# Down projection of a bidirectional encoder block: when the operands of the next item are started, and where the outputs of the upper rows stand

## The chip, the cores and the metric

The kernel runs on one core of one Trainium2 chip. The metric is device time in microseconds (us): the median of three runs, and beside it the span of one profiled execution, from its first to its last instruction. The engines are PE (matmul; PEld is its weight load), DVE (vector), ACT (scalar), POOL (GpSimd) and SP, which issues the DMAs. Each engine works through its own instructions in order; an instruction waits until the results and the buffers that it needs are released by the other engines.

## The reference, cut to what matters

One encoder layer is applied to 512 + 256 positions with the same weights. The change touches its last part, the second matrix product of the feed-forward network with the residual, and the final norm:

```
ff_gate, ff_up = jnp.split(n2 @ w_ffn_in[layer].astype(f32), 2, axis=-1)
h = h + (jax.nn.silu(ff_gate) * ff_up) @ w_ffn_out[layer].astype(f32)
...
out = _rmsnorm(h, norm_final_g)
```

Here `h` is 768 x 1024, the gated activation 768 x 2816, and `w_ffn_out` 2816 x 1024, all in float32. `_rmsnorm` divides each row by the root of its mean square and multiplies by a gain.

## The kernel before

**The product.** The 2816 inner positions are 22 blocks of 128, taken as 11 *pairs*. A pair is a 2 x 2 problem: activations a11, a12 (upper 384 rows), a21, a22 (lower 384 rows), weights b11, b12, b21, b22 (128 x 512 each). It is done with seven products instead of eight, called P2, P1, P5, P6, P3, P7, P4 in the order in which they run; most take a sum or difference of blocks as an operand, so sums are formed in place beforehand: the activation sums on POOL (`fr<-fr`, `fback<-fback`, 128 x 384), the weight sums on POOL for P5 and P4 and on DVE for P6 and P7 (`w<-w`, `wraw<-w,wraw`, 128 x 512). Pairs come in two *groups* of six and five; within a group all pairs do P2, then all do P1, and so on. One product of one pair is called an *item* here: 42 items in group 0, 35 in group 1.

**An item.** Each float32 operand is split into a high part in a shorter format and the low remainder. `operands(op)` (L2161) forms the sums and then calls `aconv` and `convert` or `staged`: ACT copies the high parts (`ahi` of the activations, `whi` of the weights), DVE subtracts to get the low parts (`alo`, `wlo`). `staged` (L2127) also has ACT copy the weights into one of two PSUM tiles (`acc<-w`), from which DVE then reads them. PE does nine matmuls per item: three row blocks i, each hi*hi, lo*hi, hi*lo (L82 to L84, or L2274 where a product adds onto earlier ones). `ahi`, `alo`, `whi`, `wlo` have rings of six buffers (AH, WH).

**The order.** `Ops(f2src(), 4)` (L2209) builds operands four items ahead of the one that PE is given: `ops.next()` hands over item n and builds item n+4. After a product's last item the sums are added to the residual rows `hres` by DVE (`accumulate`: `hres<-acc,hres`, three per product). These adds and the work on the norm stand in a queue `late`, of which up to three are emitted after each item (L2304). The upper rows (i = 0, 1, 2) are complete after P3 of group 1, the lower ones after P4. So P3 puts `upper_scales` (three squares on ACT, then a chain of seven small POOL operations that gives the scales `rstd`) and the outputs of the upper rows (`finish`, L2237) into `late`; they are emitted between the items of P7. An output piece (`yq`, 128 x 512) takes an ACT scaling and a POOL multiplication by the gain, or, where `spare` is false, one DVE operation. At the last item of P7 (`at_once`, L2296) DVE adds each row block as soon as PE has finished it, because P4 goes on in the same PSUM tiles: the first matmul of P4 has to wait for that add. P4 of group 1 runs row block by row block over its five items, and each lower row block is finished behind it.

Of the kernel before, what the change touches and what calls it, by code (L numbers as in the profile page):

```python
# [9 lines left out]
F32R = mybir.dt.float32r  # L10
I32 = mybir.dt.int32
AF = mybir.ActivationFunctionType
# [21 lines left out]
WH = 6  # L34
EARLY = (1, 2)
AH = 6
# [25 lines left out]
def build(nc, tc, I, O):  # L62
    V = nc.vector
# [4 lines left out]
    def pool(name, bufs=1, side=None, space=None):  # L68
        kw = {}
        if space is not None:  # L70
            kw["space"] = space
        if side is not None:
            kw["side"] = side
        if space is not DRAM:
            kw["reuse_waits"] = "tile"
        return tc.tile_pool(name=name, bufs=bufs, **kw)

    def raw(t):
        return t.bitcast(F32)
# [9 lines left out]
    def tt(e, out, a, b, op):  # L89
        e.tensor_tensor(out=out, in0=a, in1=b, op=op)  # L90
# [10 lines left out]
    def act(out, a, f, **kw):  # L101
        A.activation(out=out, in_=a, func=f, **kw)  # L102

    C3, C4 = P, P
    MUL, ADD, SUB = ALU.mult, ALU.add, ALU.subtract
# [3 lines left out]
    def enter(cm):  # L109
        p = cm.__enter__()  # L110
        ctx.append(cm)
        return p
# [37 lines left out]
    wk = enter(pool("wk"))  # L150
# [28 lines left out]
    class Ops:  # L179
# [10 lines left out]
        def next(self):  # L190
            self.fill(1)
            w = self.q.popleft()
            self.fill(self.ahead)
            return w
# [414 lines left out]
    rs = {}  # L609
# [735 lines left out]
    def f(n=1):  # L1345
        for _ in range(n):
            next(filler, None)
# [384 lines left out]
    for m in range(KT):  # L1732
        sga = glp.tile([128, 2, 384], F32, name="sga", tag="yr", bufs=2)
        nc.sync.dma_start(out=sga, in_=gascr[m].rearrange("p (b c) -> p b c", b=2))
        w = ws.two()
# [118 lines left out]
    for k in range(KT):  # L1854
        w = ws.next()
# [141 lines left out]
    def h12(i):  # L1997
        return hres[:, i, 512:1024]

    def h21(i):  # L2000
        return hres[:, 3 + i, 0:512]
# [82 lines left out]
    for m in range(KF):  # L2084
# [4 lines left out]
        g = gated(m, fr)  # L2089
# [10 lines left out]
    leave(n2pa_cm)  # L2100
    f2r = enter(pool("f2r", side="right"))

    def ahl():
        return [f2r.tile([128, 384], F32R, name=n, tag=n, bufs=AH) for n in ("ahi", "alo")]

    def fback():
        return f2r.tile([128, NT], F32, name="fback", tag="fback", bufs=SPILL)
# [1 line left out]
    def w21():  # L2109
        return f2r.tile([128, 1024], F32, name="w21", tag="w21", bufs=6)  # L2110

    ahl()
    fback()
    w21()

    def aconv(x, eng):
        hi, lo = ahl()
        act(hi, x, AF.Copy)
        tt(eng, lo, x, raw(hi), SUB)
        return hi, lo  # L2120

    order = list(range(SPILL // 2, KF // 2)) + list(range(SPILL // 2))
    groups = [order[0:6], order[6:11]]
    P2, P1, P5, P6, P3, P7, P4 = range(7)
    stg = []

    def staged(w):  # L2127
        hi, lo = (wk.tile([128, 512], F32R, name=n, tag=n, bufs=WH) for n in ("whi", "wlo"))
        x = stg[0]
        stg.reverse()  # L2130
        act(hi, w, AF.Copy)
        act(x, w, AF.Copy)
        tt(V, lo, x, raw(hi), SUB)
        return hi, lo

    class Pair:
        def __init__(self, p, j, last):
# [23 lines left out]
        def operands(self, op):  # L2161
            if not self.f:
                self.rows()
            (fa, fb), wa = self.f, self.w[0]
            a11, a21, a12, a22 = fa[:, 0:384], fa[:, 384:], fb[:, 0:384], fb[:, 384:]
            b11, b21 = wa[:, 0:512], wa[:, 512:]
            if len(self.w) > 1:
                b12, b22 = self.w[1][:, 0:512], self.w[1][:, 512:]
            conv = convert if op in (P2, P1, P4) else staged
            if op == P2:  # L2170
                a, b = a12, b21
                self.w.append(self.load(1))
            elif op == P1:
                a, b = a11, b11
            elif op == P5:
                if self.p == KF // 2 - 1:
                    tt(P, a21, a21, a22, ADD)
                tt(P, b12, b12, b11, SUB)
                a, b = a21, b12
            elif op == P6:  # L2180
                tt(P, a11, a21, a11, SUB)
                tt(V, b12, b22, b12, SUB)
                a, b = a11, b12
            elif op == P3:
                tt(P, a21, a12, a11, SUB)
                a, b = a21, b22
            elif op == P7:
                tt(P, a11, a22, a11, SUB)
                tt(V, b11, b12, b11, SUB)
                a, b = a11, b11  # L2190
            else:
                tt(P, b22, b21, b12, SUB)
                a, b = a22, b22
            return aconv(a, V), conv(b)

    def f2src():
        nxt = None
        for n, g in enumerate(groups):
            prs = nxt or [Pair(p, j, False) for j, p in enumerate(g)]
            for op in range(7):  # L2200
                if n == 0 and op == P6:
                    for m in range(SPILL):
                        t = fback()
                        nc.sync.dma_start(out=t, in_=ffscr[m])
                        ffs[m] = t
                for j, p in enumerate(prs):
                    yield lambda p=p, op=op: p.operands(op)
# [20 lines left out]
    fss = f2.tile([128, 12], F32, name="fss")  # L2228
# [8 lines left out]
    def finish(i, r, spare=False, qs=(0, 1)):  # L2237
        for q in qs:
            yo = row_tile()
            cs = slice(512 * q, 512 * q + 512)  # L2240
            if spare:
                act(yo, hres[:, i, cs], AF.Copy, scale=r[:, 0:1])
                tt(P, yo, yo, gfin[:, cs], MUL)
            else:
                stt(yo, hres[:, i, cs], r[:, 0:1], gfin[:, cs], MUL, MUL)
            rows_out(i, q, yo)

    def square(h, s):
        yo = f2.tile([128, 512], F32, name="yo", tag="yo", bufs=1)
        act(yo, h, AF.Square, accum_out=s)  # L2250
# [5 lines left out]
    def second_half(i, h):  # L2256
        s2 = fss[:, 6 + i:7 + i]
        square(h, s2)
        return rstd_from(fss[:, i:i + 1], s2, f2)
# [4 lines left out]
    def accumulate(op, i, ps):  # L2264
        h = uses[op](i)
        tt(V, h, ps, h, ADD)

    def product_rows(ps, i, w, fresh, k, n):
        l, r = [x[:, 128 * i:128 * i + 128] for x in w[0]], w[1]
        if fresh:  # L2270
            mm3(ps, l, r, k == 0, k == n - 1)
        else:
            for a, b in ((0, 0), (0, 1), (1, 0)):
                T.matmul(ps, l[a], r[b], start=False, stop=False, skip_group_check=True)  # L2274

    late = deque()
    rs = {}

    def upper_scales():
        for i in range(3):  # L2280
            square(h12(i), fss[:, 6 + i:7 + i])
        r = rstd_from(fss[:, 0:3], fss[:, 6:9], f2, 3)
        for i in range(3):
            rs[i] = r[:, i:i + 1]

    for g in groups:
        last = g is groups[-1]
        banks_of = {}
        for op in range(6 if last else 7):
            fresh = chain_of[op] not in banks_of  # L2290
            if fresh:
                banks_of[chain_of[op]] = [slot8(i) for i in sets[chain_of[op] == "u"]]
            accs = banks_of[chain_of[op]]
            for k in range(len(g)):
                w = ops.next()
                at_once = op == P7 and k == len(g) - 1  # L2296
                while at_once and late:
                    late.popleft()()
                for i in range(3):
                    product_rows(accs[i], i, w, fresh, k, len(g))  # L2300
                    if at_once:
                        accumulate(op, i, accs[i])
                for _ in range(min(len(late), 3)):
                    late.popleft()()  # L2304
            for i in range(3):
                if op != P7:
                    late.append(lambda op=op, i=i, ps=accs[i]: accumulate(op, i, ps))
                if last and op == P1:
                    late.append(lambda i=i: first_half(i, h11(i)))
                if last and op == P7:  # L2310
                    late.append(lambda i=i: first_half(3 + i, h22(i)))
            if last and op == P3:
                late.append(upper_scales)
                for i in range(3):
                    late.append(lambda i=i: finish(i, rs[i], spare=True, qs=(0,)))
                    late.append(lambda i=i: finish(i, rs[i], spare=i < 2, qs=(1,)))
    g = groups[-1]
    ks = [ops.next() for _ in g]
    while late:
# [1 line left out]
    for i in range(3):  # L2321
        ps = banks_of["u"][i]
        for k, w in enumerate(ks):
            product_rows(ps, i, w, False, k, len(g))
        accumulate(P4, i, ps)
        rs[3 + i] = second_half(3 + i, h21(i))
        if i == 1:
            finish(3, rs[3])
            tt(V, h22(2), h22(2), gfin[:, 512:], MUL)
        elif i == 2:  # L2330
            tt(V, h21(2), h21(2), gfin[:, 0:512], MUL)
            finish(4, rs[4])
# [107 lines left out]
```

## Time and profile before

| | us |
|---|---|
| median of 3 runs (lowest, highest) | 1336.61 (1336.58, 1336.69) |
| the profiled execution's own time | 1337.95 |
| span of the profiled execution | 1335.3 |
| PE busy in the span | 1221.5 (91%) |
| DVE busy | 959.9 (72%) |
| ACT busy | 590.7 (44%) |
| POOL busy | 652.0 (49%) |
| down projection: first to last matmul start | 1128.48 to 1326.18 |

The profiled execution took 1.34 us more than the median run, and 2.65 us of its time lie around the span. A busy PE is not a PE at its peak: matmuls overlap, and their ends are modelled, so the pace of PE is better read from the starts of its matmuls.

### The profile page before, as it was taken

The numbers are of one execution on the slowest core, as the hardware profiler recorded it, in microseconds if no ns is written. First come the engines' busy times: TensorE is split into PE (matmuls) and PEld (weight loads), VectorE is DVE, ScalarE is ACT, GpSimd is POOL, SyncE is SP. The second block draws the span as 40 slices with busy tenths as digits, with TensorE's granted clock in tenths as the row PEclk, the third lists the DMA queues.
The fourth block names the chain that finished last, engine by engine and source line by source line (L and its number), as shares of the span: only waits on it lengthen the run. The fifth ranks groups of instructions, "written<-read, shape, count | busy, mean of one in ns | idle before, by whom it ended". The sixth has DMA issues, their size and how long they took to land. (4 is left out here: it accounts for less than half of the span.)

```text
span 1335.3 us, 19177 instructions
## 1 busy us (share of the span) xinstructions
PE 1221.5 (91%) x6821; PEld 1142.2 (86%) x6821; DVE 959.9 (72%) x1587; ACT 590.7 (44%) x1235; POOL 652.0 (49%) x624
## 2 busy tenths in 40 slices
PE   7899789998999999978899998999999999998973
PEld 7789678997988989868899887999999999776852
DVE  5997997658787768898743378656665667978764
ACT  5264344634444444443332254444444444465653
POOL 4306660646676654577663047444434443732344
PEclk8899889998999999988999999999999999999997
DMA  6342357765554524305434212323222224413002
GB/s 240 77 109 64 117 150 200 175 195 166 165 171 150 167 85 148 103 32 169 136 111 153 96 48 64 130 102 101 87 76 70 77 64 147 161 45 114 1 12 83
DMA packets 74495, 152.18 MB, mean 114 GB/s; under 512 B 17808, under 2 KB 35344, under 8 KB 74400
## 3 DMA queue, kind: packets, MB, share of 16 engines
q1 hardware_dynamic: 74400, 150.97, 36.2%
q8 instruction: 53, 0.87, 0.3%
q14 instruction: 42, 0.34, 0.1%
HBM read 116.92 MB, written 34.01 MB: 113 GB/s over the span
## 5 line engine op out<-in xcount | busy, mean ns | idle before, releaser
L90 DVE TENSOR_TENSOR wlo<-wraw,whi 128x512 fp32r<-128x512 f32 x298 | 252.3, 855 | 105.2 <-ACT whi L102 105.0
L102 ACT ACTIVATE whi<-wraw 128x512 fp32r<-128x512 f32 x304 | 183.3, 623 | 62.9 <-POOL wraw L90 32.9
L90 POOL TENSOR_TENSOR wraw<-wraw 128x512 f32<-128x512 f32 x93 | 132.1, 1421 | 139.6 <-DVE wlo L90 92.7
L90 POOL TENSOR_TENSOR wraw<-wrax,wraw 128x512 f32<-128x512 f32 x38 | 51.1, 1346 | 72.3 <-DVE wlo L90 41.4
L2274 PE MATMUL acc<-whi,ahi 128*128 128x512 f32 x132 | 54.9, 416 | 23.9 <-DVE hres L90 20.1
L84 PE MATMUL bank<-n1hi,wlo 128*128 128x384 f32 x192 | 66.2, 345 | 1.7 <-DVE wlo L90 1.6
L82 PE MATMUL bank<-n1hi,whi 128*128 128x384 f32 x192 | 67.6, 352 | 0.0
L83 PE MATMUL bank<-n1lo,whi 128*128 128x384 f32 x192 | 66.3, 345 | 0.0
L82 PE MATMUL pair<-n1hi,whi 128*128 128x384 f32 (+1 forms) x168 | 60.8, 362 | 4.1 <-ACT sgst L102 4.1
L102 ACT ACTIVATE q<-bank 128x384 f32<-128x384 f32 x80 | 38.2, 484 | 52.5 <-PE bank L84 48.8
L83 PE MATMUL pair<-n1lo,whi 128*128 128x384 f32 (+1 forms) x168 | 58.5, 348 | 0.0
L84 PE MATMUL pair<-n1hi,wlo 128*128 128x384 f32 (+1 forms) x168 | 58.1, 346 | 0.0
L2274 PE MATMUL acc<-wlo,ahi 128*128 128x512 f32 x132 | 55.0, 417 | 2.5 <-DVE wlo L90 2.5
L90 DVE TENSOR_TENSOR wlo<-wrax,whi 128x512 fp32r<-128x512 f32 x50 | 44.0, 886 | 15.8 <-ACT whi L102 15.8
L2274 PE MATMUL acc<-whi,alo 128*128 128x512 f32 x132 | 54.3, 411 | 0.0
L2274 PEld LDWEIGHTS acc<-whi,ahi 128*128 128x128 f32 x132 | 26.2, 198 | 31.9 <-issue 20.5
L102 ACT ACTIVATE whi<-w 128x512 fp32r<-128x512 f32 x59 | 36.6, 621 | 29.3 <-DVE w L90 20.6
L90 DVE TENSOR_TENSOR X<-X,single 128x128 f32<-128x128 f32 (+2 forms) x128 | 42.9, 335 | 4.4
L90 POOL TENSOR_TENSOR fr<-fr 128x384 f32<-128x384 f32 x29 | 36.4, 1260 | 17.4 <-DVE alo L90 16.8
L90 POOL TENSOR_TENSOR er<-pwF,Cc 128x512 f32<-128x512 f32 x8 | 8.9, 1114 | 72.7 <-DVE pwF L567 43.3
L83 PE MATMUL bank<-yTlo,whi 128*128 128x384 f32 x128 | 43.0, 336 | 1.5 <-DVE yTlo L90 1.5
L84 PE MATMUL bank<-yThi,wlo 128*128 128x384 f32 x128 | 43.0, 336 | 0.8 <-DVE wlo L90 0.8
(525 smaller groups left out, 4340.0 us busy)
## 6 DMA issues: line engine op xcount, KB each, us to landing
wraw<-in_wfi SPq DMA_DIRECT2D x35, 512.0 KB, 3.6
wraw<-in_win SPq DMA_DIRECT2D x33, 512.0 KB, 5.3
w<-in_wfo SPq DMA_DIRECT2D x16, 512.0 KB, 5.3
wrax<-in_win SPq DMA_DIRECT2D x11, 512.0 KB, 4.3
wrax<-in_wfi SPq DMA_DIRECT2D x11, 512.0 KB, 3.6
fb<-fbscr SPq DMA_DIRECT2D x8, 512.0 KB, 5.3
wraw<-in_wo SPq DMA_DIRECT2D x8, 512.0 KB, 3.7
ffscr<-fr SPq DMA_DIRECT2D x10, 384.0 KB, 3.0
```

The source lines that it names most:

```text
L82: T.matmul(out, l[0], r[0], start=start, stop=False)
L83: T.matmul(out, l[0], r[1], start=False, stop=False)
L84: T.matmul(out, l[1], r[0], start=False, stop=stop)
L90: e.tensor_tensor(out=out, in0=a, in1=b, op=op)
L102: A.activation(out=out, in_=a, func=f, **kw)
L2274: T.matmul(ps, l[a], r[b], start=False, stop=False, skip_group_check=True)
```

## The change

The operands of an item are now built in two steps. `halves_of` (new) does the ACT copies at once, behind the sums that `operands` forms, and returns a function `rest` that does the two DVE subtractions later. `f2src` begins item n+1 (sums and ACT copies) and only then finishes item n (low parts). In P4 of group 0 the weights are now also copied into the PSUM tiles (six more ACT copies); before, P4 was not staged.

At the end, `late` keeps only the three squares of the upper rows behind P3. The POOL chain and the six output pieces of the upper rows are emitted after the matmuls of row block 0 of P4, behind all operands; row block 0 goes from ACT and POOL to DVE, and row block 2 goes wholly to DVE.

```diff
-    def aconv(x, eng):
-        hi, lo = ahl()
-        act(hi, x, AF.Copy)
-        tt(eng, lo, x, raw(hi), SUB)
-        return hi, lo
...
-    def staged(w):
-        hi, lo = (wk.tile([128, 512], F32R, name=n, tag=n, bufs=WH) for n in ("whi", "wlo"))
-        x = stg[0]
-        stg.reverse()
-        act(hi, w, AF.Copy)
-        act(x, w, AF.Copy)
-        tt(V, lo, x, raw(hi), SUB)
-        return hi, lo
+    def halves_of(a, w, stage):
+        ahi = f2r.tile([128, 384], F32R, name="ahi", tag="ahi", bufs=AH)
+        whi = wk.tile([128, 512], F32R, name="whi", tag="whi", bufs=WH)
+        act(ahi, a, AF.Copy)
+        act(whi, w, AF.Copy)
+        x = w
+        if stage:
+            x = stg[0]
+            stg.reverse()
+            act(x, w, AF.Copy)
+
+        def rest():
+            alo = f2r.tile([128, 384], F32R, name="alo", tag="alo", bufs=AH)
+            wlo = wk.tile([128, 512], F32R, name="wlo", tag="wlo", bufs=WH)
+            tt(V, alo, a, raw(ahi), SUB)
+            tt(V, wlo, x, raw(whi), SUB)
+            return (ahi, alo), (whi, wlo)
+
+        return rest
...
-            conv = convert if op in (P2, P1, P4) else staged
+            stage = op not in (P2, P1) and (op != P4 or self.p in groups[0])
...
     def f2src():
-        nxt = None
+        it = f2items()
+        begun = [next(it)()]
+
+        def one():
+            f = next(it, None)
+            begun.append(f and f())
+            return begun.pop(0)()
+
+        for _ in range(7 * len(order)):
+            yield one
...
             if last and op == P3:
-                late.append(upper_scales)
-                for i in range(3):
-                    late.append(lambda i=i: finish(i, rs[i], spare=True, qs=(0,)))
-                    late.append(lambda i=i: finish(i, rs[i], spare=i < 2, qs=(1,)))
+                late.append(lambda: [square(h12(i), fss[:, 6 + i:7 + i]) for i in range(3)])
...
+        if i == 0:
+            upper_scales()
+            finish(1, rs[1], spare=True)
+            finish(0, rs[0], qs=(0,))
         accumulate(P4, i, ps)
         rs[3 + i] = second_half(3 + i, h21(i))
+        if i == 0:
+            finish(0, rs[0], qs=(1,))
+            finish(2, rs[2])
```

What this moves on the engines shows at three places. On DVE, in group 0 where P5 ends and P6 begins, before (`w_11489` and `w_11502` are b12 of the first two pairs, the `acc` of the `wlo` rows are the two PSUM tiles):

```order
L90 TENSOR_TENSOR hres<-acc_11669,hres 128x512
L90 TENSOR_TENSOR hres<-acc_11670,hres 128x512
L90 TENSOR_TENSOR alo<-fr,ahi 128x384
L90 TENSOR_TENSOR wlo<-acc_11553,whi 128x512
L90 TENSOR_TENSOR w_11489<-w_11489 128x512
L90 TENSOR_TENSOR alo<-fr,ahi 128x384
L90 TENSOR_TENSOR wlo<-acc_11552,whi 128x512
L90 TENSOR_TENSOR w_11502<-w_11502 128x512
```

and at the same place in the changed kernel, where `w_11495` is b12 of the second pair:

```order
L90 TENSOR_TENSOR hres<-acc_11673,hres 128x512
L90 TENSOR_TENSOR hres<-acc_11674,hres 128x512
L90 TENSOR_TENSOR w_11489<-w_11489 128x512
L90 TENSOR_TENSOR alo<-fr,ahi 128x384
L90 TENSOR_TENSOR wlo<-acc_11559,whi 128x512
L90 TENSOR_TENSOR w_11495<-w_11495 128x512
L90 TENSOR_TENSOR alo<-fr,ahi 128x384
L90 TENSOR_TENSOR wlo<-acc_11558,whi 128x512
```

Each weight sum has moved ahead of the low parts of the item before it, so two subtractions now lie between a sum and the low part that is made from it.

On POOL, at the end of group 1 in P7, of the change against before (rows with `w_...<-` are the weight sums of P4, `fss` and `rvar` to `rstd` are the small operations of the scales, `yq` the gain of the outputs):

```order
+L90 TENSOR_TENSOR w_12345<-wraw,w_12345 128x512
+L90 TENSOR_TENSOR w_12364<-wraw,w_12364 128x512
+L90 TENSOR_TENSOR w_12383<-w_12322,w_12383 128x512
+L90 TENSOR_TENSOR w_12402<-w_12324,w_12402 128x512
+L96 TENSOR_SCALAR fss<-fss 128x1 x3
 L94 TENSOR_SCALAR rvar<-fss 128x3
 L90 TENSOR_TENSOR rvar<-rvar,fss 128x3
```

and, four rows of the same chain further on:

```order
 L90 TENSOR_TENSOR rstd<-rstd,rtmp 128x3
 L90 TENSOR_TENSOR yq<-yq,gffn 128x512 x2
-L90 TENSOR_TENSOR w_12352<-wraw,w_12352 128x512
-L90 TENSOR_TENSOR yq<-yq,gffn 128x512 x3
-L90 TENSOR_TENSOR w_12371<-wraw,w_12371 128x512
-L90 TENSOR_TENSOR w_12390<-w_12329,w_12390 128x512
-L90 TENSOR_TENSOR w_12412<-w_12331,w_12412 128x512
-L96 TENSOR_SCALAR fss<-fss 128x1 x3
```

Four of the five sums of P4 stood behind the chain of the upper scales and behind output pieces; now all five stand ahead of them, and three of the five POOL pieces are gone.

On DVE at the very end of the changed kernel, from the adds of P7 on (the `yq` rows are output pieces):

```order
L90 TENSOR_TENSOR hres<-acc_12514,hres 128x512
L90 TENSOR_TENSOR alo<-fback,ahi 128x384
L90 TENSOR_TENSOR wlo<-w_12402,whi 128x512
L99 SCALAR_TENSOR_TENSOR yq<-hres,rstd,gffn 128x512
L90 TENSOR_TENSOR hres<-acc_12512,hres 128x512
L99 SCALAR_TENSOR_TENSOR yq<-hres,rstd,gffn 128x512 x3
L90 TENSOR_TENSOR hres<-acc_12513,hres 128x512
L99 SCALAR_TENSOR_TENSOR yq<-hres,rstd,gffn 128x512 x2
```

The first and the next three `yq` are upper pieces; in the kernel before, one upper piece is on DVE, between low parts of P4, and none stands between the adds of the three row blocks.

## Rows read from the trace of the kernel before

**Rows 1.** Windows, three stages: length, busy PE, PEld, DVE, ACT, POOL; clock, DMA, GB/s.
```profile
1128.48:1313.82 185.34, 158.45 (x649) 123.18 (x649) 147.50 (x209) 103.68 (x207) 86.21 (x73) 0.94 0.21 76
1313.82:1326.58 12.76, 12.75 (x45) 9.85 (x45) 5.42 (x9) 3.57 (x10) 4.42 (x11) 0.83 0.10 38
1326.58:1335.30 8.72, 0.00 (x0) 0.00 (x0) 3.20 (x5) 1.44 (x3) 3.25 (x8) 0.80 0.34 125
```

**Rows 2.** Timeline of PE, down projection: start, duration, matmul, [idle before it <- releaser].
```profile
1128.48 0.39 PE L82 MATMUL acc<-whi,ahi 128*128 128x512 f32 x1
...
1154.67 0.39 PE L82 MATMUL acc<-whi,ahi 128*128 128x512 f32 x1
...
1180.20 0.49 PE L2274 MATMUL acc<-whi,ahi 128*128 128x512 f32 x1 [0.99 <-ACT whi L102]
...
1197.57 0.40 PE L2274 MATMUL acc<-whi,ahi 128*128 128x512 f32 x1
...
1214.50 0.47 PE L2274 MATMUL acc<-whi,ahi 128*128 128x512 f32 x1 [2.83 <-ACT whi L102]
...
1228.76 0.40 PE L82 MATMUL acc<-whi,ahi 128*128 128x512 f32 x1
...
1260.38 0.40 PE L2274 MATMUL acc<-whi,ahi 128*128 128x512 f32 x1
...
1313.82 0.77 PE L2274 MATMUL acc<-whi,ahi 128*128 128x512 f32 x1 [20.08 <-DVE hres L90]
...
1317.37 0.63 PE L2274 MATMUL acc<-whi,alo 128*128 128x512 f32 x1
...
1326.18 0.40 PE L2274 MATMUL acc<-whi,alo 128*128 128x512 f32 x1
```

**Rows 3.** Timeline of all engines, from P7 to P4 of group 1.
```profile
1297.94 2.80 POOL L90 TENSOR_TENSOR yq<-yq,gffn 128x512 f32<-128x512 f32 x2 [0.83 <-ACT yq L102]
...
1303.32 4.02 POOL L90 TENSOR_TENSOR yq<-yq,gffn 128x512 f32<-128x512 f32 x3 [1.35 <-ACT yq L102]
...
1307.30 1.26 POOL L90 TENSOR_TENSOR w<-wraw,w 128x512 f32<-128x512 f32 x1
...
1310.26 1.75 DVE L99 SCALAR_TENSOR_TENSOR yq<-hres,rstd,gffn 128x512 f32<-128x512 f32 x1
...
1313.00 1.87 DVE L90 TENSOR_TENSOR hres<-acc,hres 128x512 f32<-128x512 f32 x3
```

**Rows 4.** Timeline of POOL, the chain of the upper scales.
```profile
1294.51 0.25 POOL L94 TENSOR_SCALAR rvar<-fss 128x3 f32<-128x3 f32 x1 [18.56 <-ACT yo L102]
...
1296.91 0.20 POOL L90 TENSOR_TENSOR rstd<-rstd,rtmp 128x3 f32<-128x3 f32 x1
```

**Rows 5.** Timelines of DVE, ACT and POOL: one item of P6, group 0.
```profile
1171.81 0.68 DVE L90 TENSOR_TENSOR w<-w 128x512 f32<-128x512 f32 x1
1172.40 0.55 DVE L90 TENSOR_TENSOR alo<-fr,ahi 128x384 fp32r<-128x384 f32 x1
1173.76 0.69 DVE L90 TENSOR_TENSOR wlo<-acc,whi 128x512 fp32r<-128x512 f32 x1 [0.80 <-ACT acc L102]
1174.37 0.68 DVE L90 TENSOR_TENSOR w<-w 128x512 f32<-128x512 f32 x1
...
1172.60 0.63 ACT L102 ACTIVATE whi<-w 128x512 fp32r<-128x512 f32 x1 [0.99 <-DVE w L90]
1173.14 0.58 ACT L102 ACTIVATE acc<-w 128x512 f32<-128x512 f32 x1
...
1173.10 1.02 POOL L90 TENSOR_TENSOR fr<-fr 128x384 f32<-128x384 f32 x1 [1.53 <-DVE alo L90]
```

**Rows 6.** Timelines of DVE and POOL: DVE beside POOL in P5, group 0.
```profile
1156.03 1.05 DVE L90 TENSOR_TENSOR alo<-fr,ahi 128x384 fp32r<-128x384 f32 x1
...
1155.65 1.02 POOL L90 TENSOR_TENSOR fr<-fr 128x384 f32<-128x384 f32 x1 [0.56 <-DVE alo L90]
```

**Rows 7.** Timelines of DVE and ACT before the down projection starts on PE.
```profile
1126.23 1.07 DVE L90 TENSOR_TENSOR alo<-fr,ahi 128x384 fp32r<-128x384 f32 x1 [1.00 <-ACT ahi L102]
...
1125.26 0.53 ACT L102 ACTIVATE sB<-c 128x384 f32<-128x384 f32 x1 [2.71 <-DVE c L90]
```

More of the change, by code (lines that the diff above doesn't have):

```diff
@@ L2101, in build @@
     f2r = enter(pool("f2r", side="right"))
-    def ahl():
-        return [f2r.tile([128, 384], F32R, name=n, tag=n, bufs=AH) for n in ("ahi", "alo")]
+    for n in ("ahi", "alo"):
+        f2r.tile([128, 384], F32R, name=n, tag=n, bufs=AH)
     def fback():
@@ L2110, in w21 @@
         return f2r.tile([128, 1024], F32, name="w21", tag="w21", bufs=6)
-    ahl()
     fback()
     w21()
-    def aconv(x, eng):
-        hi, lo = ahl()
-        act(hi, x, AF.Copy)
-        tt(eng, lo, x, raw(hi), SUB)
-        return hi, lo
     order = list(range(SPILL // 2, KF // 2)) + list(range(SPILL // 2))
@@ L2193, in operands, with f2items @@
                 a, b = a22, b22
-            return aconv(a, V), conv(b)
+            return halves_of(a, b, stage)
     def f2src():
-        nxt = None
+        it = f2items()
[6 more added lines that the diff above has]
+            yield one
+    def f2items():
         for n, g in enumerate(groups):
-            prs = nxt or [Pair(p, j, False) for j, p in enumerate(g)]
+            prs = [Pair(p, j, False) for j, p in enumerate(g)]
             for op in range(7):
@@ L2279, in upper_scales @@
     def upper_scales():
-        for i in range(3):
-            square(h12(i), fss[:, 6 + i:7 + i])
         r = rstd_from(fss[:, 0:3], fss[:, 6:9], f2, 3)
@@ L2312, in build @@
             if last and op == P3:
-                late.append(upper_scales)
-                for i in range(3):
-                    late.append(lambda i=i: finish(i, rs[i], spare=True, qs=(0,)))
-                    late.append(lambda i=i: finish(i, rs[i], spare=i < 2, qs=(1,)))
+                late.append(lambda: [square(h12(i), fss[:, 6 + i:7 + i]) for i in range(3)])
     g = groups[-1]
```

## The prediction

> **What bounds the kernel now.** I read the table of stages first. In the 185.34 us from the first matmul of the down projection to the first of its P4 in group 1, PE is busy for 158.45 us, so it stands idle for 26.89 us; P4 then takes 12.76 us at a mean granted clock of 0.83, and 8.72 us lie behind the last matmul [rows 1]. PE works through the up projection before this without such gaps, so only this stage is in play.
>
> The timeline of PE says what the stage costs without waits. Fifteen items of group 1 (P2, P1, P5) start at 1228.76 and end at 1260.38: 2.108 us an item [rows 2]. Measured against that, from starts in the same rows:
>
> - P2 and P1, group 0 (12 items): 26.19 us instead of 25.30, lost 0.89.
> - P5, P6, P3, group 0 (18): 42.90 instead of 37.95, lost 4.95.
> - P7 and P4, group 0 (12): 31.19 instead of 25.30, lost 5.89.
> - P2 to P5, group 1: nothing.
> - P6, P3, P7, group 1 (15): 53.44 instead of 31.62, lost 21.82, of which 20.08 is one wait in front of P4.
> - P4, group 1 (5): 12.76 instead of 10.54, lost 2.22.
>
> The total is 35.8 us; 26.9 is idle time, and the other 8.9 is matmuls that step more slowly behind the long gaps, at the lower of the two levels of the clock (1.2 and 2.4 GHz).
>
> The big wait is followed backwards on all engines. It ends with the adds `hres` on DVE at 1313.00 [rows 3]. In front of these, in DVE's order, stand the low parts of four items of P4 and one output piece, which starts at 1310.26 and takes 1.75 us. The low parts wait for ACT, ACT for POOL's weight sums, and the sums (the one at 1307.30 is an example) stand behind output pieces that hold POOL from 1297.94 and from 1303.32 [rows 3]. The chain of the upper scales, ahead of them all, itself waited 18.56 us for the squares [rows 4]. PE had run dry 20.08 us before, at 1293.7, so the operands of P4 are late by the length of an output stage that no operand needs.
>
> The smaller losses have another shape. In P6 a weight sum on DVE (0.68 us) is followed by ACT's two copies (0.63 and 0.58), and DVE, after the 0.55 us of `alo`, waits 0.80 us for the second copy; ACT in its turn waits 0.99 us for the next sum [rows 5]. Sum to sum this is 1171.81 to 1174.37: 2.56 us for an item, slower than PE's 2.108. The lead of the operands shrinks by 0.45 us an item until PE stands, as at 1180.20. P7 has the same chain. At 1214.50 the named releaser is an ACT copy [rows 2], but the wait is that for the adds of P7, in the same place in the program as the 20 us one.
>
> **The change, part by part.**
>
> *Sums and copies ahead of low parts (P5 to P3, group 0).* Without the wait, DVE needs per item what its rows step by: 0.59 (sum to `alo`), 0.46 for `alo` and 0.61 (`wlo` to next sum), 1.66 us. But POOL's `fr` sum of 1.02 us now runs while DVE is at work, not while it waits. What that does is seen in P5: `alo` takes 1.05 us beside a POOL sum instead of 0.55, and ends 0.41 after it, [rows 6]; `wlo`, whose weights come from PSUM, keeps its 0.69 beside the same kind of sum (1173.76 beside 1173.10 [rows 5]). In P6 the POOL sum starts 0.70 us after `alo` does [rows 5], so it is the next weight sum that meets it, ends some 0.5 us behind it, and the step becomes 2.2 us. That is within 0.1 of PE's 2.108: five steps and the three adds of P5 (1.87 us, as in [rows 3]) cost 2.3 us of lead, and I estimate 1 to 2 us at the start of P6, 1 of it from the next term. I leave 0.5 us of the loss: -4.45. Bounds: nothing left, -4.95; POOL adding its 0.5 us to a second operation of each item, half of the loss kept, -2.5. The Trainium skill, page "SBUF — State Buffer", section "SBUF: two separate sides", says that a DVE operation with two SBUF inputs and a GpSimd operation exclude each other for a whole instruction. By that rule the sum would start only when POOL is done and take its full 0.68, a step of 2.35 us, and the term would be -3.7; it speaks against this part of the change, and the trace agrees in kind ([rows 6]), with 0.14 us less (0.41 behind POOL instead of 0.55).
>
> *The start (P2, P1, group 0).* Before PE starts, DVE waits 1.00 us for `ahi`, which stands on ACT behind `sB`, and `sB` waited 2.71 us [rows 7]. In the new order this `ahi` is ahead of `sB`. DVE then runs on without waits, beside POOL's sums, up to the two stalls at the end of P1, so 1 us earlier covers the 0.89: -0.89. Bounds: 0 and -0.89.
>
> *P7 and P4, group 0.* In P7 POOL has no sums left that wait for DVE, so DVE steps at 1.66 and gains 0.44 us an item on PE; the sum pipeline removes the stalls inside P7. The first matmul of P4 still waits for adds behind four items of low parts, 4 x (0.46 + 0.61) = 4.3 us or, each `alo` 0.5 longer beside POOL's sums for group 1, up to 6.3. I keep 1.9 us of 5.89 (a gap near 1 us and some slow matmuls): -4.0. Bounds -5.9 and -1.5. The six added ACT copies (0.58 each, 3.5 us) are hidden in the time that ACT has free, 82 of the first 185 us [rows 1]; without that cover they would cost 3.5.
>
> *Group 1 up to P4.* With the chain and the pieces out of P7, POOL forms all five sums behind its `fback` sums; 5 x 1.26 us, ended well before P7 does. What remains in front of P4 is, as in group 0, the adds of P3, four items of low parts, and the adds of P7. I keep 0.8 us: -21.0. Bounds -21.8, and -16 if the squares, still on ACT ahead of the third item's copies, and POOL's sums make P4 six late.
>
> *P4.* Without the long gap its 45 matmuls go at the pace of the rest: -2.2, bounds -2.2 and 0.
>
> *The tail.* The upper outputs now lie here. Covered by row block 0's matmuls (3.5 us) is the chain, 2.60 us [rows 4]. Then DVE has, between the adds of the three lower blocks, four upper pieces (0.75 us alone, 1.75 beside POOL [rows 3]) and two of row block 3; POOL has two pieces, 2.80 us, in front of the chain for block 3. The last add was at once behind the last matmul before (8.72 us to the end [rows 1]). I count pieces 0,0 before add 0; 0,1, 2,0 and 2,1 before add 1, two of them beside POOL, 4 us where PE gives 3.5; the chain for block 3 behind POOL's pieces, then two pieces and a multiplication before add 2. That comes out 2.9 us behind the last matmul: +2.9. Bounds +1 (POOL never in the way) and +6 (every piece 1.75). The same twelve transfers go out; none of the six moved ones is the last.
>
> Sum: -4.45 - 0.89 - 4.0 - 21.0 - 2.2 + 2.9 = -29.6. The span would be 1335.3 - 29.6 = 1305.7, the execution 1337.95 - 29.6 = 1308.3. Against the median, 1.34 us lower, it is **1307.0**. All good ends give -34.8 (1301.8), all bad ones -14.0 (1322.6).
>
> **The rivals.**
>
> 1. *DVE beside POOL becomes the bound.* The gaps that go from DVE were where POOL ran. If POOL's sums hit both DVE operations from SBUF in an item, the step is 1.66 + 1.0 = 2.7 us, above the 2.56 of now. For: `alo` at 1.05 [rows 6]. Against: the staged low parts are not hit. Then the 4.95, the 0.89 and most of the 5.89 stay: 1336.6 - 21.0 - 2.2 + 2.9 + 1 (P7 of group 1 likewise) = 1317. That the reordering does nothing, because ACT cannot run ahead, gives 1316 likewise; the 0.99 us that ACT waits for DVE's sum [rows 5] speaks against it.
> 2. *The tail is dearer.* POOL's and DVE's pieces and the chains take turns, so that the adds and the three chains queue up: +9 instead of +2.9, 1313. For: DVE's in-order pieces ahead of each add. Against: POOL's share falls from five pieces to two.
> 3. *Slower.* The eight steps behind the long wait take 3.55 us, 0.44 each, where the pace is 2.108 / 9 = 0.234 [rows 2]: at the lower level an item costs 1.8 us more. If PE now met a gap near 1 us in nearly every item, as at 1180.20 [rows 2], the level could stay low through P6, P7 and P4. From 17 such items on, the gain of 29.6 is gone; all 33 of them would give 1307 + 33 x 1.8 = 1366. Against: an item's step comes down to PE's, and a lone 0.99 us gap costs far less.
>
> **How the numbers follow.** Forecast 0.60 (own range 1302.5 to 1312), rival 1 with its twin 0.20, rival 2 0.14, rival 3 0.02, and 0.04 for a stay of the long wait in some form (around 1325). The range 1302 to 1318 takes in the bounds of the forecast's terms and the first two rivals; it leaves out the long wait's stay, rival 3, and something at each end. A run of this kernel tells 0.2%, 2.7 us, from no change. All cases but rival 3 and half of the last are faster: 0.96 faster, 0.02 same, 0.02 slower.
>
> **What would show it.** Right: the idle 20 us in front of P4 of group 1 is under 2; sum to sum in P6 about 2.2 us with no wait of `wlo` for `acc`; P7 without a wait; the last add 2 to 4 us behind the last matmul. Wrong: a wait on DVE's adds in front of either P4 above 3 us, a P6 step above 2.5, or more than 13 us from the last matmul to the end.

## The result, and the profile after

The changed kernel takes 1307.01 us (median of 4 runs, 1305.62 to 1307.67), beside 1336.59 us for the kernel before in the same comparison (1333.79 to 1336.69): a ratio of 0.9782 with a 95% interval of 0.9765 to 0.9799. The forecast was 1307.0. That the two agree to a hundredth is luck, as the terms below show; that it lies well inside the range is not.

The stages of the down projection after, in the columns of [rows 1] (first matmul to the first of P4 in group 1, P4, from the end of the last matmul to the end):

```profile
1130.78:1283.37 152.59, 151.97 (x649) 121.89 (x649) 140.25 (x207) 103.70 (x207) 77.31 (x60) 1.00 0.24 82
1283.37:1294.16 10.79, 10.78 (x45) 8.37 (x45) 7.74 (x10) 4.18 (x10) 7.82 (x15) 1.00 0.16 59
1294.16:1305.70 11.54, 0.00 (x0) 0.00 (x0) 5.13 (x8) 2.17 (x5) 5.43 (x13) 0.61 0.59 218
```

The first stage has shrunk from 185.34 to 152.59 us, and PE stands idle in it for 0.62 us instead of 26.89. The granted clock is 1.00 in it and in P4, where it was 0.94 and 0.83. P4 is 1.97 us shorter; the part behind the last matmul has grown from 8.72 to 11.54 us.

The timeline of PE after, for [rows 2], shows where the items start:

```profile
1130.78 0.39 PE L82 MATMUL acc<-whi,ahi 128*128 128x512 f32 x1
...
1156.07 0.39 PE L82 MATMUL acc<-whi,ahi 128*128 128x512 f32 x1
...
1168.72 0.40 PE L2289 MATMUL acc<-whi,ahi 128*128 128x512 f32 x1
...
1194.02 0.40 PE L2289 MATMUL acc<-whi,ahi 128*128 128x512 f32 x1
...
1219.33 0.40 PE L82 MATMUL acc<-whi,ahi 128*128 128x512 f32 x1
...
1250.96 0.39 PE L2289 MATMUL acc<-whi,ahi 128*128 128x512 f32 x1
...
1283.37 0.47 PE L2289 MATMUL acc<-whi,ahi 128*128 128x512 f32 x1 [0.62 <-DVE hres L90]
```

P2 and P1 of group 0 take 25.29 us, P5, P6 and P3 37.95, P7 and P4 25.31: at 2.108 us an item all three are at the pace, to 0.01 us. The only row with an idle time in the whole stage is the one at 1283.37.

P6 in group 0, for [rows 5], on DVE, ACT and POOL: the sum and the `alo` of its first step, then one whole step:

```profile
1159.18 1.06 DVE L90 TENSOR_TENSOR w<-w 128x512 f32<-128x512 f32 x1
1160.17 1.37 DVE L90 TENSOR_TENSOR alo<-fr,ahi 128x384 fp32r<-128x384 f32 x1
...
1162.06 1.18 DVE L90 TENSOR_TENSOR w<-w 128x512 f32<-128x512 f32 x1
1163.17 0.55 DVE L90 TENSOR_TENSOR alo<-fr,ahi 128x384 fp32r<-128x384 f32 x1
1163.64 0.68 DVE L90 TENSOR_TENSOR wlo<-acc,whi 128x512 fp32r<-128x512 f32 x1
1164.24 1.19 DVE L90 TENSOR_TENSOR w<-w 128x512 f32<-128x512 f32 x1
...
1165.54 0.63 ACT L102 ACTIVATE whi<-w 128x512 fp32r<-128x512 f32 x1 [0.61 <-DVE w L90]
...
1147.54 13.59 POOL L90 TENSOR_TENSOR fr<-fr 128x384 f32<-128x384 f32 x11
1161.68 1.01 POOL L90 TENSOR_TENSOR fr<-fr 128x384 f32<-128x384 f32 x1 [0.56 <-DVE alo L90]
1163.86 1.01 POOL L90 TENSOR_TENSOR fr<-fr 128x384 f32<-128x384 f32 x1 [1.16 <-DVE alo L90]
```

From the second step on, sum to sum is 2.18 us, without a wait on DVE. The weight sum meets POOL's sum and takes 1.18 us instead of 0.68; `alo` and `wlo` are not touched. The first step is longer, 2.88 us from 1159.18 to 1162.06: POOL is still in a row of eleven sums without a pause, up to 1161.13, and both the weight sum (1.06) and `alo` (1.37) meet it. ACT, at work one item ahead, waits for DVE's sums, and nobody waits for ACT here.

POOL in P7 and P4 of group 1, for [rows 3] and [rows 4], and the end on DVE, from the same timeline:

```profile
1263.25 4.61 POOL L90 TENSOR_TENSOR w<-wraw,w 128x512 f32<-128x512 f32 x3
1267.81 3.32 POOL L90 TENSOR_TENSOR w<-w,w 128x512 f32<-128x512 f32 x2
...
1284.13 0.19 POOL L96 TENSOR_SCALAR fss<-fss 128x1 f32<-128x1 f32 x1 [13.00 <-ACT yo L102]
...
1285.89 0.25 POOL L94 TENSOR_SCALAR rvar<-fss 128x3 f32<-128x3 f32 x1
...
1288.51 0.75 DVE L99 SCALAR_TENSOR_TENSOR yq<-hres,rstd,gffn 128x512 f32<-128x512 f32 x1 [3.02 <-POOL rstd L90]
...
1289.31 3.00 POOL L90 TENSOR_TENSOR yq<-yq,gffn 128x512 f32<-128x512 f32 x2 [0.83 <-ACT yq L102]
1289.78 3.75 DVE L99 SCALAR_TENSOR_TENSOR yq<-hres,rstd,gffn 128x512 f32<-128x512 f32 x3
...
1297.05 0.68 DVE L90 TENSOR_TENSOR hres<-acc,hres 128x512 f32<-128x512 f32 x1
```

All five sums of P4 are done at 1271.1, 12 us before P4 begins. POOL then stands for 13.00 us, and its chain for the upper rows runs only behind the three `fss` operations of the lower rows. DVE waits 3.02 us for that chain, and the last add starts at 1297.05, 2.9 us behind the end of the last matmul.

### The profile page after: what moved, and what is told of

Its sections match the earlier page's. It is cut to its first block, busy times and chain, and to the rows that moved or that the text cites. A ratio compares the mean times of both kernels' runs of the same rounds, so it can differ in the third digit from the quotient of the medians.

```text
span 1305.7 us, 19189 instructions
## 1 busy us (share of the span) xinstructions
PE 1214.7 (93%) x6821; PEld 1142.3 (87%) x6821; DVE 957.6 (73%) x1590; ACT 591.7 (45%) x1238; POOL 648.4 (50%) x621
## 5 line engine op out<-in xcount | busy, mean ns | idle before, releaser
L90 DVE TENSOR_TENSOR wlo<-wraw,whi 128x512 fp32r<-128x512 f32 x298 | 246.7, 836 | 104.9 <-ACT whi L102 104.0
L2289 PE MATMUL acc<-wlo,ahi 128*128 128x512 f32 x132 | 52.3, 396 | 0.0
L82 PE MATMUL bank<-yThi,whi 128*128 128x384 f32 x128 | 42.9, 335 | 0.0
L82 PE MATMUL pair<-whi,n1hi 128*128 128x256 f32 x144 | 41.2, 286 | 0.0
```

Source lines behind the costliest of these rows:

```text
L82: T.matmul(out, l[0], r[0], start=start, stop=False)
```

## The experiments

Two theories stood against each other at the start. The first: the change consists of two parts with separate gains, the order of the operands (group 0) and the place of the outputs (the long wait of group 1). The rival: one part gives nearly all, and the other is idle. Later runs asked what the longer tail and the DVE operations beside POOL cost. All stages below are read as in [rows 1], since the start of the down projection differs from one execution to the next.

| kernel | median, us | start | to P4 of group 1 | P4 | behind | together |
|---|---|---|---|---|---|---|
| before | 1336.61 | 1128.48 | 185.34 | 12.76 | 8.72 | 206.82 |
| before, again | 1337.07 | 1132.65 | 185.38 | 12.32 | 8.75 | 206.45 |
| changed | 1307.01 | 1130.78 | 152.59 | 10.79 | 11.54 | 174.92 |
| changed, again | 1306.99 | 1130.44 | 152.61 | 10.78 | 11.57 | 174.96 |
| look-ahead alone | 1318.07 | 1129.96 | 163.97 | 12.61 | 8.66 | 185.24 |
| outputs alone | 1324.78 | 1131.16 | 171.21 | 12.33 | 10.00 | 193.54 |
| P4 not staged | 1307.44 | 1133.90 | 152.56 | 10.77 | 11.57 | 174.90 |
| one POOL sum more | 1308.08 | 1131.59 | 153.58 | 10.78 | 11.65 | 176.01 |
| two POOL sums more | 1311.07 | 1130.48 | 155.89 | 10.77 | 11.76 | 178.42 |
| early chain | 1303.69 | 1128.82 | 152.60 | 10.78 | 9.80 | 173.18 |
| early chain, all on DVE | 1303.57 | 1127.89 | 152.61 | 10.78 | 9.12 | 172.51 |

**1. The look-ahead alone.** The changed kernel with the squares, the scales and the pieces of the upper rows back behind P3:

```diff
...
-                late.append(lambda: [square(h12(i), fss[:, 6 + i:7 + i]) for i in range(3)])
+                late.append(upper_scales)
+                for i in range(3):
+                    late.append(lambda i=i: finish(i, rs[i], spare=True, qs=(0,)))
+                    late.append(lambda i=i: finish(i, rs[i], spare=i < 2, qs=(1,)))
...
```

> The look-ahead alone: operands of the next item begun early, as in the changed kernel, but the upper rows' squares, scales and six output pieces back behind P3 of group 1, between the items of P7, as before. My theory (two separate gains, one for each part of the change): the losses of P2 to P4 in group 0 go (0.9 + 5.0 + 5.9 = 11.7 us), the last add is again at once behind the last matmul (8.7 us to the end), and POOL's sums for P4 still stand behind the chain and the pieces, so that PE still waits in front of P4 of group 1, though the first two sums are now a place further ahead: 11 to 14 us idle there; about 1318. Rival (the long wait stays whole, 20 us, since the sums of the last three items still follow all POOL pieces): about 1324. Second rival (the order of the operands gave it all, the place of the outputs nothing): about 1307.

Measured: 1318.07 us (1315.70 to 1319.33), ratio 0.9853 (0.9834 to 0.9871). Its timeline has a single idle time on PE, and in front of it, on POOL and DVE:

```profile
1285.62 4.57 POOL L90 TENSOR_TENSOR yq<-yq,gffn 128x512 f32<-128x512 f32 x3 [1.35 <-ACT yq L102]
...
1290.15 2.48 POOL L90 TENSOR_TENSOR w<-w,w 128x512 f32<-128x512 f32 x2
1291.44 0.63 ACT L102 ACTIVATE whi<-w 128x512 fp32r<-128x512 f32 x1 [4.27 <-POOL w L90]
...
1292.10 1.08 DVE L90 TENSOR_TENSOR wlo<-w,whi 128x512 fp32r<-128x512 f32 x1 [4.25 <-ACT whi L102]
...
1293.11 1.88 DVE L90 TENSOR_TENSOR hres<-acc,hres 128x512 f32<-128x512 f32 x3
...
1293.93 0.77 PE L2289 MATMUL acc<-whi,ahi 128*128 128x512 f32 x1 [12.01 <-DVE hres L90]
```

The losses of group 0 are all gone, and the wait in front of P4 has shrunk to 12.01 us, with two sums ahead of the pieces instead of one. It is still the same wait: POOL's pieces, then the sums, ACT's copy, DVE's low part, the adds. The first theory holds, the rivals do not.

**2. The place of the outputs alone.** The kernel before, with only the edits at the end:

```diff
...
-                late.append(upper_scales)
-                for i in range(3):
-                    late.append(lambda i=i: finish(i, rs[i], spare=True, qs=(0,)))
-                    late.append(lambda i=i: finish(i, rs[i], spare=i < 2, qs=(1,)))
+                late.append(lambda: [square(h12(i), fss[:, 6 + i:7 + i]) for i in range(3)])
...
+        if i == 0:
+            upper_scales()
+            finish(1, rs[1], spare=True)
+            finish(0, rs[0], qs=(0,))
...
+        if i == 0:
+            finish(0, rs[0], qs=(1,))
+            finish(2, rs[2])
```

> The place of the outputs alone: operands in the order of the kernel before, four items ahead, but the upper rows' scales and pieces behind the last operands, as in the changed kernel. My theory: the losses in group 0 stay as they were (0.9 + 5.0 + 5.9 = 11.7 us), in group 1 P6 to P7 lose what they lost apart from the long wait (1.7 us), and the wait in front of P4 falls from 20 us to 3 to 5 us, like the one in front of P4 of group 0; the tail is that of the changed kernel, 2.8 us longer than before: about 1322. Rival (the long wait was also fed by the operand order, so it stays near 10 us without the look-ahead): about 1328. Second rival (the end alone gives nearly everything): about 1309.

Measured: 1324.78 us (1321.57 to 1326.49), ratio 0.9897 (0.9875 to 0.9918). The larger idle times of PE in group 0 and the one in front of P4, and DVE ahead of that one:

```profile
1182.89 0.50 PE L2274 MATMUL acc<-whi,ahi 128*128 128x512 f32 x1 [1.00 <-ACT whi L102]
...
1211.02 0.49 PE L2274 MATMUL acc<-whi,ahi 128*128 128x512 f32 x1 [1.01 <-ACT whi L102]
...
1217.21 0.77 PE L2274 MATMUL acc<-whi,ahi 128*128 128x512 f32 x1 [2.84 <-ACT whi L102]
...
1302.37 0.75 PE L2274 MATMUL acc<-whi,ahi 128*128 128x512 f32 x1 [5.22 <-DVE hres L90]
...
1289.15 0.69 DVE L90 TENSOR_TENSOR wlo<-acc,whi 128x512 fp32r<-128x512 f32 x1 [0.80 <-ACT acc L102]
...
1301.54 1.88 DVE L90 TENSOR_TENSOR hres<-acc,hres 128x512 f32<-128x512 f32 x3
```

The waits of group 0 are those of the kernel before to 0.02 us ([rows 2]; the one at 1211.02 has its like, 1.00, in the second trace of the kernel before); the long one is 5.22 us, a little above the 3 to 5 expected. So the outputs alone take 14.9 us off the 20.08, the look-ahead alone 8.1, and both together 19.5. In the 5.22 us that the outputs alone leave, DVE comes to the adds late: in P7 it waits four times 0.80 us for ACT's copy into PSUM, and once more 0.45 us before P4. In the changed kernel the waits in P7 are gone. The two gains overlap, since both shorten the same wait: 21.6 and 13.3 us in the stages, but 31.9 together. The time is 2.8 us above the 1322 expected. The part behind the last matmul grew by only 1.3 us, to 10.00, and not by the 2.8 expected: the last add comes 13.68 us behind the first matmul of P4 here and in the changed kernel alike, but P4 itself lasts 12.33 us here instead of 10.79.

**3. P4 of group 0 without the copies into PSUM.**

```diff
-            stage = op not in (P2, P1) and (op != P4 or self.p in groups[0])
+            stage = op not in (P2, P1, P4)
```

> The changed kernel, but P4 of group 0 is not staged (no copies of its weights into the PSUM tiles; DVE reads the weights from SBUF). Theory A (the low parts from PSUM are what keeps DVE clear of POOL's sums for group 1 there): some of the six low parts take about 0.5 us more, at most 3 us in all, and DVE, which had waited 0.73 us for PE ahead of the adds of P7, becomes late by 1 to 2 us there; the time is 1307 to 1309. Theory B (the lead of 3 to 4 us covers it): the rows get longer, PE has no new gap, 1306.5 to 1307.5. Rival (the staging gave the whole gain of P4 in group 0): a gap of 2.8 us in front of P4 again, 1311 or more.

Measured: 1307.44 us (1305.62 to 1310.62), ratio 0.9751 (0.9724 to 0.9778); the stages are those of the changed kernel to 0.03 us. Theory B: the six copies make no difference to the time. One of the six low parts, now read from SBUF, does meet a POOL sum for group 1 and takes 1.73 us instead of 0.69; DVE's wait for PE ahead of the adds of P7 shrinks from 0.73 to 0.17 us, and PE has no gap there:

```profile
1206.68 1.73 DVE L90 TENSOR_TENSOR wlo<-w,whi 128x512 fp32r<-128x512 f32 x1
1208.59 2.10 DVE L90 TENSOR_TENSOR hres<-acc,hres 128x512 f32<-128x512 f32 x3 [0.17 <-PE acc L2289]
...
1206.39 1.48 POOL L90 TENSOR_TENSOR w<-w,wraw 128x512 f32<-128x512 f32 x1 [17.65 <-DMA w<-in_wfo]
```

So the copies do keep a low part clear of POOL, as theory A had it; the lead covers what that is worth, with 0.17 us left.

**4. The chain early.** The changed kernel with the chain of the upper scales moved into POOL's 13 us of idle time:

```diff
+                if last and at_once:
+                    upper_scales()
...
         if i == 0:
-            upper_scales()
             finish(1, rs[1], spare=True)
```

> The changed kernel with the POOL chain of the upper scales emitted right behind the operands of the last item, in the 13 us in which POOL stands idle ahead of its last small operations; the output pieces stay where they are. Theory A (the tail is 2.8 us longer than before because the upper pieces on DVE wait for the chain at the start of P4: DVE stood 3.0 us for it): the upper pieces start some 4 us earlier, DVE is clear before row block 0 ends, the last add comes at once behind the last matmul, and the 11.5 us from there to the end become 8.7 to 9.5: about 1304.5. Theory B (the tail is set by POOL and DVE taking turns on the pieces and by the chain of block 3 that stands behind POOL's pieces): within 0.7 us of the changed kernel, 1306.3 to 1307.0.

Measured: 1303.69 us (1302.92 to 1305.94), ratio 0.9750 (0.9734 to 0.9766); beside it the changed kernel again:

> The changed kernel once more, as the measure for the others on the same chip: 1307 by any theory, with the last add 2.9 us behind the last matmul. Its profile tells whether the 2.3 us by which the down projection started later than in the profile of before, behind code that the change does not touch, belong to the kernel (start near 1130.8 again) or to the execution (start anywhere from 1128.5 to 1130.8).

That one took 1306.99 us (1303.08 to 1308.40), ratio 0.9767 (0.9746 to 0.9788). The two intervals overlap, and of the 3.3 us between the medians only 1.8 lie in the stages: in the profiles the part behind the last matmul is 9.80 us instead of 11.57, while the start of the down projection, which the edit does not touch, differs by 1.6. In that part theory A holds, though 9.80 lies above its 8.7 to 9.5, and the last add is still 1.1 us late. The chain did not run as it was meant to:

```profile
1277.81 2.96 POOL L94 TENSOR_SCALAR rvar<-fss 128x3 f32<-128x3 f32 x1 [8.63 <-ACT yo L102]
...
1279.99 0.68 DVE L90 TENSOR_TENSOR wlo<-w,whi 128x512 fp32r<-128x512 f32 x1
1280.60 1.87 DVE L90 TENSOR_TENSOR hres<-acc,hres 128x512 f32<-128x512 f32 x3
...
1282.36 1.23 POOL L90 TENSOR_TENSOR rtmp<-rtmp,rvar 128x3 f32<-128x3 f32 x1
...
1282.86 0.68 DVE L90 TENSOR_TENSOR wlo<-w,whi 128x512 fp32r<-128x512 f32 x1
...
1285.81 4.00 DVE L99 SCALAR_TENSOR_TENSOR yq<-hres,rstd,gffn 128x512 f32<-128x512 f32 x3
```

The first operation, 0.25 us in the changed kernel, takes 2.96 us here and ends when DVE passes from its low parts of P4 to the adds; another takes 1.23 us and ends with a low part. Measured from the first matmul of P4, the chain starts 6.1 us earlier than in the changed kernel (3.6 us ahead of it instead of 2.5 behind), but the pieces only 2.4 us earlier (2.8 us behind it instead of 5.1).

**5. The early chain, and the upper pieces all on DVE.** On top of the last one:

```diff
-            finish(1, rs[1], spare=True)
+            finish(1, rs[1])
```

> As the kernel with the early chain, and row block 1, whose two pieces went over ACT and POOL, goes to DVE like the other upper rows: six pieces on DVE, none on POOL. Theory A (what is left of the longer tail comes from POOL's pieces: beside them three DVE pieces take 4.00 us instead of about 2.1, and the chain of block 3 stands behind them): the six pieces take 6 x 0.68 = 4.1 us, the chain of block 3 ends before DVE gets to it, the last add comes within 0.3 us of the last matmul's end instead of 1.1 us behind it, and the time falls by 0.5 to 1.2 us against the kernel with the early chain, to about 1302.8. Rival (the number of pieces on DVE sets the tail, not POOL): two pieces more, 1.4 us, so the last add is 2.5 us behind the last matmul: about 1305.

Measured: 1303.57 us (1302.18 to 1305.33), ratio 0.9727 (0.9704 to 0.9751). The six pieces, in two groups:

```profile
1283.27 2.08 DVE L99 SCALAR_TENSOR_TENSOR yq<-hres,rstd,gffn 128x512 f32<-128x512 f32 x3 [0.65 <-POOL rstd L90]
...
1285.87 2.07 DVE L99 SCALAR_TENSOR_TENSOR yq<-hres,rstd,gffn 128x512 f32<-128x512 f32 x3
...
1289.80 1.42 DVE L99 SCALAR_TENSOR_TENSOR yq<-hres,rstd,gffn 128x512 f32<-128x512 f32 x2 [1.26 <-POOL rstd L96]
```

Six pieces take 4.15 us here, where three took 4.00 beside POOL. The part behind the last matmul falls by 0.68 us to 9.12, within 0.4 of the kernel before: theory A. DVE still waits 1.26 us for the chain of block 3, which was to end before DVE gets to it, so the last add is 0.46 us late rather than under 0.3. The medians of this kernel and the last one cannot be told apart, so that the gain of 0.68 us rests on the stages.

**6 and 7. More of POOL beside DVE.** The changed kernel with one, or two, further POOL sums in each item of P6 in group 0, into a tile that nothing reads:

```diff
...
                 tt(P, a11, a21, a11, SUB)
+                if self.p in groups[0]:
+                    for _ in range(1):
+                        tt(P, scr, a12, a22, ADD)
```

> The changed kernel with one further POOL sum of 128 x 384 per item of P6 in group 0 (a sum of two activation blocks into a scratch tile that nothing reads). It doubles what DVE meets of POOL there. Theory A (each POOL sum holds up one DVE operation from SBUF by about 0.5 us): the step of P6 goes from 2.18 to about 2.7 us, as in rival 1 of the prediction. The operands of the first item of P6 are 4.4 us ahead of PE, and five steps take 3.0 us of that: no gap or one below 0.5 us, 1307 to 1307.5. Theory B (as rival 1 put it, such a step makes DVE the bound at once): gaps of 0.6 us in most items, slower matmuls behind them, 1310 or more. Theory C (a second sum finds DVE in its PSUM operations and costs nothing): the step stays below 2.3.

> The same with two further POOL sums per item of P6 in group 0. Theory A: the step is 2.18 + 2 x 0.5 = 3.2 us, which is also about what three sums of 1.02 us take on POOL; five steps and the adds of P5 use up 5.5 to 6 us against a lead of 4.4 us, so PE stands for 1.5 to 2.5 us around the end of P6, and some matmuls behind it go slowly: 1309 to 1311. Theory B (DVE is the bound from the first such item): 6 x 1.1 = 6.6 us and slow matmuls, 1314 or more. Theory C (POOL's sums give way to DVE): the step stays below 2.5, 1307.

Measured: 1308.08 us (1305.94 to 1310.58) and 1311.07 us (1308.90 to 1311.63), ratios 0.9761 (0.9735 to 0.9787) and 0.9780 (0.9757 to 0.9803). Run 3, which has the stages of the changed kernel, took 1307.44 us beside the same executions of the kernel before, so by the time alone run 6 cannot be told from it, and the stages decide. One step of P6 with one sum more, and PE's only idle time there:

```profile
1165.38 0.90 DVE L90 TENSOR_TENSOR w<-w 128x512 f32<-128x512 f32 x1
1166.21 1.37 DVE L90 TENSOR_TENSOR alo<-fr,ahi 128x384 fp32r<-128x384 f32 x1
1167.50 0.68 DVE L90 TENSOR_TENSOR wlo<-acc,whi 128x512 fp32r<-128x512 f32 x1
1168.10 0.91 DVE L90 TENSOR_TENSOR w<-w 128x512 f32<-128x512 f32 x1
...
1180.90 0.51 PE L2293 MATMUL acc<-wlo,ahi 128*128 128x512 f32 x1 [0.41 <-DVE wlo L90]
```

The first step is 2.89 us, as long as without the added sums; the next three are 2.72 us, theory A's figure, and the last two 2.18 again, by when POOL is through with the added sums. It costs 0.41 us of idle time in P6 and 1.1 us in the three stages together. With two sums the step is 3.00 us once and then stays at 2.72 to the end of P6; it does not become 3.2. POOL is then never idle, both of DVE's operations from SBUF meet a sum in each item, and an item has no third one: theory A was right for one added sum and wrong for two. PE stands for 1.47 us in P6 and for 0.81 in front of P4 of group 0, 2.3 us together and within theory A's 1.5 to 2.5, and the three stages together are 3.5 us longer. In neither run was DVE the bound from the first item on: the lead was used up first.

**8. The kernel before once more.**

> The kernel before once more, with a profile, for what the first experiments left open: the down projection of the changed kernels began at 1127.9 to 1133.9 us in their profiles, that of the kernel before at 1128.48 in the only profile of it. Theory A (this start scatters from execution to execution in both kernels): it may lie anywhere from 1127 to 1134, and from it to the end of the span 206.8 us pass again, within 0.5. Theory B (the changed kernels start 2 us later for a reason of their own): 1128.5 within 0.5.

Measured: 1337.07 us (1335.50 to 1340.83), ratio 0.9997 (0.9984 to 1.0010). Its down projection starts at 1132.65, and the span ends 206.45 us later, with 20.05 us of idle time in front of P4. Theory A: the start scatters in both kernels, 1128.5 to 1132.7 in two executions of the one and 1127.9 to 1133.9 in nine of the others. Where in the part ahead of it the time goes was not looked into.

## Why the prediction was right, point by point

Measured from the starts of the matmuls and the stages above, before against after:

| term | forecast | measured |
|---|---|---|
| the start, P2 and P1 | -0.89 | -0.90 |
| P5, P6, P3, group 0 | -4.45 | -4.95 |
| P7, P4, group 0 | -4.0 | -5.88 |
| group 1 up to P4 | -21.0 | -21.0 |
| P4 | -2.2 | -2.0 |
| tail | +2.9 | +2.8 |
| sum | -29.6 | -31.9 |

The three stages together fell by 31.9 us, and the span by 29.6, because in the profile of the changed kernel the part ahead of it, which the change does not touch, was 2.30 us longer (1130.78 against 1128.48). Run 8 shows this as scatter. The sum was therefore 2.3 us too small, and the scatter gave it back. Beside the medians of the kernel before that were taken with them, the changed kernel was 29.6 and 30.2 us faster, and run 3, with the same stages, 33.0; the times scatter by as much as the starts do.

- *The start.* Right in size. The `alo` that waited 1.00 us for `ahi` in [rows 7] follows at once on DVE in the changed kernel (at 1127.45), and the stall at the end of P1 is gone; that the first alone did away with the second was not tried by itself.
- *Sums and copies ahead of low parts.* The step of 2.2 us was right from the second one on (2.18), and so was the place: POOL's sum meets the weight sum of DVE, which takes 0.5 us longer. The first step, 2.88 us, is above the 2.5 that the prediction named as a sign of being wrong, and has the form of rival 1, both operations from SBUF held up; PE does not notice it. In the later steps, as in [rows 6], DVE's operation ended sooner than a full wait for POOL would let it: the weight sum 0.55 us behind POOL's end, where it takes 0.68 alone. By the rule of the Trainium skill (page "SBUF — State Buffer", section "SBUF: two separate sides") the step would be 2.35 us, as the prediction estimated. The trace agrees with that rule in kind, with a step 0.17 us shorter. What was mis-sized is "I leave 0.5 us of the loss". The operands of P6's first item were ready at 1164.32 and its matmul started at 1168.72: 4.4 us of lead, not the 1 to 2 that the prediction estimated. Four steps at 0.07 us over PE's pace and the adds of P5 take 1.05 us of it: the operands of the last item of P6 were ready at 1175.91, and its matmul started at 1179.26 (timelines of DVE and PE after). The prediction had counted 2.3 us for that.
- *P7 and P4, group 0.* This is the term that was off: "I keep 1.9 us of 5.89". The estimate let the adds of P7 stand behind four late items of low parts, each `alo` lengthened by a POOL sum. In the trace DVE is early instead. It waits for PE ahead of these adds, 0.73 us, and POOL's sums for group 1 wait for their weights until 1202.09. With no gap in P4, no slow matmuls follow.

```profile
1202.09 1.29 POOL L90 TENSOR_TENSOR w<-w,wraw 128x512 f32<-128x512 f32 x1 [16.49 <-DMA w<-in_wfo]
...
1205.47 2.10 DVE L90 TENSOR_TENSOR hres<-acc,hres 128x512 f32<-128x512 f32 x3 [0.73 <-PE acc L2289]
```

- *Group 1 up to P4.* Right in size and mechanism. Runs 1 and 2 share it out: the pieces on POOL were the larger part of the 20 us, and the rest needed both edits.
- *P4.* The granted clock stays at 1.00, as in runs 3 to 7, where the wait in front of P4 is 0.59 to 0.64 us; in runs 1 and 2, behind waits of 12.01 and 5.22 us, it is 0.84 and 0.86, and P4 takes 12.61 and 12.33 us. In the changed kernel, though, this gain does not reach the end of the span: P4 and the part behind it take 22.33 us together both there and in run 2, since the last add comes 13.68 us behind the start of P4 in both. The prediction added -2.2 and +2.9 as if each stood for itself; with the outputs behind P4, DVE sets the end and not PE.
- *The tail.* The amount was right, the account only in part, so the agreement of +2.8 with +2.9 is partly luck. The chain for block 3 did stand behind POOL's pieces, and DVE's pieces did take 1.25 us each beside them. But the chain of the upper scales was counted as covered by row block 0, and it stands behind the three `fss` operations, which wait for ACT's squares of the lower rows; DVE lost 3.02 us there. In run 4 that chain ends 2.7 us behind the start of P4, about where the prediction had put it, and the last add is then 1.1 us late and not 2.9. So what the prediction counted is worth 1.1 us, and what it left out 1.8. Run 4 takes the second away, run 5 most of the first, and together they give back 2.4 of the 2.8 us.
- *Rival 1.* Its step of 2.7 us was made in P6 of group 0: in three more items in run 6, in all of them in run 7. That cost 1.1 and 3.5 us, where the rival kept 4.95 us for P5 to P3 alone: DVE slower than PE for a few items is a matter of lead before it is a bound. Its other places, P7 and group 1, were not given such steps in any run. *Rival 2* fell with a last add 2.9 us behind the last matmul, *rival 3* with a clock of 1.00.

## What to carry to other kernels

A pipeline of sums, copies and low parts that is begun one item earlier cost nothing here, because ACT and DVE had the time. What it saves is seen in the lead of the operands over PE: work that out in us (4.4 here) before calling a slower step a loss. Output work that no operand needs belongs behind the last operand on every in-order engine that it uses. Its small scalar chains can go into an idle stretch ahead of that; look at what else in the queue stands ahead of them, and at what the other engines do in that stretch. Where upstream code scatters by some us, compare the stage, not the span.

## What was unexpected

Small POOL operations were held up beside DVE: 2.96 us for one of 128 x 3 that takes 0.25 us elsewhere, until DVE, which had been running low parts from SBUF without a pause, turned to operations that read PSUM (run 4; the same 2.96 us in run 5). That `rvar` waited for DVE's use of SBUF is read from the two ends in the timeline and was not tried by itself. In the other direction, with POOL's 128 x 384 sums back to back, DVE's two operations from SBUF took 0.90 and 1.37 us instead of 0.68 and 0.55, and no more when a third sum was added (runs 6 and 7). Beside a 128 x 512 sum a single one took 1.73 us (run 3).
